# SyncE's branch to the program's end, moved ahead of its wait for the stores

## Chip, cores, metric

One core of a Trainium2 chip. The metric is the device time of the launch in microseconds (us). The kernel before takes 161.09 us (median of 3 runs, 161.05 to 161.20).

## The reference

```python
# x: float32 [32, 512, 1024]
relu_x = np.maximum(x, 0)
return np.mean(relu_x, axis=-1).astype(np.float32)      # [32, 512]
```

16384 rows of 1024 numbers: 67.11 MB are read, 64 KB are written.

## The kernel before

Each of the 128 partitions has 128 rows, of which 127 go through the main loop and one is done first, on its own. SyncE issues all loads; ScalarE and VectorE share the rows (each takes max(x, 0) and the sum in one instruction); GpSimd scales the sums; SyncE issues three stores, which all count up one semaphore, `stored`, by 16 each. The end that the change touches:

```python
    nc.sync.wait_ge(pool, 2)
    nc.sync.dma_start(out=outr[:, :j0], in_=res[:, :j0]).then_inc(stored, 16)
    nc.sync.wait_ge(dve, n_done + 2)
    nc.sync.wait_ge(pool, 4)
    nc.sync.dma_start(out=outr[:, j0:], in_=res[:, j0:]).then_inc(stored, 16)

    used = [s.num for s in (*loaded, act, dve, pool, first)]
    assert used == list(range(used[0], used[0] + len(used)))
    nc.sync.sem_clear(range(used[0], used[-1] + 1))
    nc.sync.wait_ge(stored, 48).then_inc(stored, -48)

    for e, hint in zip(hinted, hints):           # ScalarE and VectorE
        e.br_lt(flag, 1, on_true="rows_begin", on_false="rows_end").branch_hint(hint)
    nc.br("rows_end", engines=[e for e in mybir.ALL_ENGINES if e not in (h.engine for h in hinted)])
    nc.switch_bb("rows_end")
```

A program is written in blocks, and `br` is a branch to a block. Block `rows_end` follows `rows_begin` directly and is empty.

Of the kernel before, what the change touches and what calls it, by code (L numbers as in the profile page):

```python
# [25 lines left out]
def issue_ahead_of_entry_barrier(nc, n):  # L26


    entry = nc.cur_f.blocks[0].instructions
    for _ in range(n):  # L30
        body, load = next(
            (block.instructions, k)
            for block in nc.cur_f.blocks[1:]
            for k, ins in enumerate(block.instructions)
            if ins.opcode == "DMACopy"
        )
        first = body[load]
        assert first.engine == mybir.EngineType.SP and not first.sync_info.on_wait
        assert all(i.opcode in ("Drain", "EventSemaphore") or i.engine != first.engine for i in body[:load])
        del body[load]  # L40
        at = next(k for k, i in enumerate(entry) if i.engine == first.engine and i.opcode == "Drain")
        entry.insert(at, first)
# [3 lines left out]
def kernel(  # L46
# [10 lines left out]
    nc = tc.nc  # L57
# [38 lines left out]
    stored = nc.alloc_semaphore("stored")  # L96
# [115 lines left out]
    used = [s.num for s in (*loaded, act, dve, pool, first)]  # L212
    assert used == list(range(used[0], used[0] + len(used)))
    nc.sync.sem_clear(range(used[0], used[-1] + 1))
    nc.sync.wait_ge(stored, 48).then_inc(stored, -48)

    for e, hint in zip(hinted, hints):
        e.br_lt(flag, 1, on_true="rows_begin", on_false="rows_end").branch_hint(hint)
    nc.br("rows_end", engines=[e for e in mybir.ALL_ENGINES if e not in (h.engine for h in hinted)])
    nc.switch_bb("rows_end")  # L220

    issue_ahead_of_entry_barrier(nc, 2)

# [29 lines left out]
```

## Time and profile before

| | us |
|---|---|
| median of three runs | 161.09 |
| profiled run, device time | 161.36 |
| profiled run, span of the trace | 160.01 |
| of it up to the issue of the last store | 158.54 |
| from there to the end of SyncE's wait for the stores | 1.47 |

The span runs from the first to the last instruction of the kernel. The device time is longer by what follows: in the trace's semaphore records, semaphore 2 is counted up at 158.09, 158.26 and 158.67 us, and again from 160.15 us, 0.136 us after the end of SyncE's wait, to 161.458 us. I call this the closing barrier: its second part begins only when SyncE has passed its wait, in every run below. The device time is 0.095 to 0.109 us less than the last count in each profiled run of this study (161.36 here). So the time of a run is taken apart below as **the issue of the last store + the tail up to the barrier's last count - 0.10 us**; the tail of before is 161.458 - 158.543 = 2.915 us. The profile's lines for this kernel stand in the prediction.

### The profile page before, as it was taken

The page shows a single profiled execution, that of the slowest core. Times are in us where ns is not written, and L with a number is a line of the kernel's source. Part 1 is how long each engine was busy: PE and PEld are TensorE (multiplying, and loading weights), DVE is VectorE, ACT ScalarE, POOL GpSimd, SP SyncE. Part 2 cuts the span into 40 slices and gives each one's busy share as a digit, 9 for nine tenths or more (in the row PEclk, how much of TensorE's full clock was granted, in tenths as well). Part 3 has the DMA queues.
Part 4 walks back from the last instruction along what each step waited for, and adds up shares of the span by engine and source line. Part 5 has one row for each costly group of instructions (what it writes and reads, how often), then busy time and mean ns, then how long its engine had stood idle before and what let it go on. Part 6 is the DMA issues. An engine that isn't in the chain of part 4 may idle for free.

```text
span 160.0 us, 350 instructions
## 1 busy us (share of the span) xinstructions
DVE 73.5 (46%) x133; ACT 70.3 (44%) x133; POOL 1.3 (1%) x9
## 2 busy tenths in 40 slices
DVE  0000029900498005970079500894009920199975
ACT  1400029800497005950079300892009900199974
POOL 1000000000000000000000000000000000000001
DMA  9969979999799699699699699699896996989993
GB/s 393 508 279 524 459 328 524 393 393 524 311 475 524 262 524 524 262 524 524 262 524 524 262 524 524 262 524 426 360 524 262 524 524 262 477 366 460 403 411 128
DMA packets 2456, 67.18 MB, mean 420 GB/s; under 512 B 536, under 2 KB 792, under 8 KB 1176
## 3 DMA queue, kind: packets, MB, share of 16 engines
q1 hardware_dynamic: 2456, 67.18, 97.9%
HBM read 67.11 MB, written 0.07 MB: 420 GB/s over the span
## 4 chain that ended last, share of the span: by engine, by line
DMA 84%; DVE 12%; SPq 1%; issue 1%; ACT 0%; DVEq 0%
DMA rows<-in_x_dram 56%; DMA last<-in_x_dram 29%; DVE rows L20 12%; SPq L109 1%; ACT last L15 0%; DVE last L199 0%; DVEq L198 0%; SPq L115 0%
## 5 line engine op out<-in xcount | busy, mean ns | idle before, releaser
L20 DVE TENSOR_SCALAR_CACHE_REDUCE rows<-rows 128x1024 f32<-128x1024 f32 (+1 forms) x63 | 72.1, 1208 | 78.8 <-DMA rows<-in_x_dram 78.6
L15 ACT ACTIVATE rows<-rows 128x1024 f32<-128x1024 f32 x64 | 66.2, 1036 | 84.0 <-DMA rows<-in_x_dram 83.8
L15 ACT ACTIVATION_READ_ACCUMULATOR rows<-rows 128x1 f32 x64 | 12.0, 187 | 0.0
L20 DVE DVE_READ_ACCUMULATOR rows<-rows 128x1 f32 x63 | 5.2, 83 | 0.0
L168 DVE STREAM_TRANSPOSE turned<-mean 128x32 f32<-128x32 f32 x1 | 0.2, 213 | 6.1 <-ACT row L164 6.1
L164 ACT ACT_TABLE_LOAD x1 | 1.3, 1283 | 3.5 <-DMA row<-in_x_dram 3.5
L157 POOL TENSOR_SCALAR res<-sums 128x112 f32<-128x112 f32 (+1 forms) x2 | 0.5, 247 | 154.0 <-DVE rows L20 154.0
L164 ACT ACTIVATE row<-row 128x1024 f32<-128x1024 f32 x1 | 1.1, 1057 | 0.0
L20 DVE TENSOR_SCALAR_CACHE_REDUCE last<-last 128x128 f32<-128x128 f32 (+1 forms) x2 | 0.6, 318 | 0.0
L15 ACT ACTIVATE last<-last 128x448 f32<-128x448 f32 x1 | 0.6, 576 | 0.1
L199 DVE SCALAR_TENSOR_TENSOR last<-last,scale 128x259 f32<-128x259 f32 x1 | 0.4, 429 | 0.1
L142 POOL MEMSET scale<- 128x259 f32 x1 | 0.3, 314 | 0.0
L187 POOL TENSOR_SCALAR res<-part 128x1 f32<-128x1 f32 x1 | 0.3, 264 | 0.6 <-DVE rows L20 0.6
L164 ACT ACTIVATION_READ_ACCUMULATOR row<-row 128x1 f32 x1 | 0.2, 187 | 0.0
L15 ACT ACTIVATION_READ_ACCUMULATOR last<-last 128x1 f32 x1 | 0.2, 186 | 0.0
L20 DVE DVE_READ_ACCUMULATOR last<-last 128x1 f32 x2 | 0.2, 82 | 0.0
L141 POOL MEMSET mean<- 128x32 f32 x1 | 0.1, 124 | 1.5 <-POOLq L55 1.5
L237 POOL MEMSET const-bfloat16-1.0<- 128x1 bf16 x1 | 0.1, 101 | 0.0
L237 POOL MEMSET const-uint8-127<- 128x1 uint8 x1 | 0.1, 101 | 0.0
L237 POOL MEMSET const-float32-0.0<- 128x1 f32 x1 | 0.1, 98 | 0.2 <-issue 0.2
L237 POOL MEMSET const-float32-1.0<- 128x1 f32 x1 | 0.1, 99 | 0.0
L199 DVE DVE_READ_ACCUMULATOR last<-last,scale 128x1 f32 x1 | 0.1, 84 | 0.0
## 6 DMA issues: line engine op xcount, KB each, us to landing
rows<-in_x_dram SPq DMA_DIRECT2D x1, 3584.0 KB, 38.1
rows<-in_x_dram SPq DMA_DIRECT2D x1, 2048.0 KB, 42.6
rows<-in_x_dram SPq DMA_DIRECT2D x1, 1024.0 KB, 44.7
row<-in_x_dram SPq DMA_DIRECT2D x1, 512.0 KB, 3.4
rows<-in_x_dram SPq DMA_DIRECT2D x1, 512.0 KB, 45.4
last<-in_x_dram SPq DMA_DIRECT2D x1, 288.0 KB, 45.7
last<-in_x_dram SPq DMA_DIRECT2D x1, 128.0 KB, 45.4
rows<-in_x_dram SPq DMA_DIRECT2D x7, 48.8
```

Source lines behind the costliest of these rows:

```text
L15: return nc.scalar.activation(out=src, in_=src, func=ACT.Relu, accum_out=acc)
L20: return nc.vector.tensor_scalar(out=src, in0=src, scalar1=0.0, scalar2=init, op0=ALU.max, op1=ALU.add, accum_out=acc,)
L109: nc.sync.dma_start(out=dst, in_=src).then_inc(loaded[i], 16)
L141: nc.gpsimd.memset(mean0[:, :], 0.0)
L142: nc.gpsimd.memset(scale[:, :], inv).then_inc(pool, 1)
L157: nc.gpsimd.tensor_scalar(out=res[:, lo:hi], in0=sums[:, lo:hi], scalar1=inv, scalar2=0.0, op0=ALU.mult, op1=ALU.add,).then_inc(pool, 1)
L164: nc.scalar.activation(out=row0[:, :], in_=row0[:, :], func=ACT.Relu, scale=inv, accum_out=mean0[:, 0:1],).then_inc(first, 1)
L168: nc.vector.transpose(turned0[:, :], mean0[:, :]).then_inc(first, 1)
L187: nc.gpsimd.tensor_scalar(out=res[:, J - 2:J - 1], in0=part[:, 0:1], scalar1=part[:, 1:2], scalar2=inv, op0=ALU.add, op1=ALU.mult,).then_i ...
L199: nc.vector.scalar_tensor_tensor(out=last[:, 768:], in0=last[:, 768:], scalar=0.0, in1=scale[:, :], op0=ALU.max, op1=ALU.mult, accum_out=r ...
L237: nc = _bacc.Bacc("TRN2", target_bir_lowering=False, num_devices=1)
```

## The change

Its intent: SyncE has about 1 us to wait for its stores. If it branches to the program's end ahead of that wait, whatever the branch costs should lie under the wait.

```diff
     nc.sync.sem_clear(range(used[0], used[-1] + 1))
-    nc.sync.wait_ge(stored, 48).then_inc(stored, -48)
 
     for e, hint in zip(hinted, hints):
         e.br_lt(flag, 1, on_true="rows_begin", on_false="rows_end").branch_hint(hint)
     nc.br("rows_end", engines=[e for e in mybir.ALL_ENGINES if e not in (h.engine for h in hinted)])
     nc.switch_bb("rows_end")
+    nc.sync.wait_ge(stored, 48).then_inc(stored, -48)
```

## The prediction

The forecast's sum is 161.09 - 0.01 = 161.08 us, the 0.01 being taken out of the 0 to 0.03 us that the trace's gaps give for the border. From the trace's gaps alone, (a) is at most 0.03 us (an estimate: 60 - 29 ns). The 1.35 us outside the span is 161.36 - 160.01.

> **What bounds the kernel now.** I read the page first, its chain of waits and its DMA lines:
>
> ```profile
> span 160.0 us, 350 instructions
> DVE 73.5 (46%) x133; ACT 70.3 (44%) x133; POOL 1.3 (1%) x9
> ...
> q1 hardware_dynamic: 2456, 67.18, 97.9%
> HBM read 67.11 MB, written 0.07 MB: 420 GB/s over the span
> ...
> DMA 84%; DVE 12%; SPq 1%; issue 1%; ACT 0%; DVEq 0%
> ```
>
> The reader should see a program bound by its loads. The two computing engines are busy under half of the span (46% and 44%), the DMA engines 97.9% of it, and the chain that ends last is 84% DMA. Nothing in the change touches a load, so the only place where it can act is the tail. So the next view is the same chain in order of time, last pieces only (start, length, what):
>
> ```profile
> 111.55 45.74 DMA last<-in_x_dram
> 157.29 0.02 issue
> 157.31 0.06 ACT last L15
> 157.37 0.42 issue
> 157.79 0.20 ACT last L15
> 157.99 0.04 DVEq L198
> 158.03 0.04 issue
> 158.08 0.12 DVE last L199
> 158.19 0.24 issue
> 158.43 0.08 DVE last L199
> ```
>
> The last loads land about 157.3 us (those that the end hangs on), VectorE finishes the last sum at 158.51, and then comes SyncE alone. What SyncE does from there stands in the stretch of the last instructions, in the list of its waits and in the records of its wait line:
>
> ```profile
> 158.54 0.34 SPq L210 DMA_DIRECT2D out_dram<-res  x1
> ...
> SPq L215 <- SPq L215: 1.0, 1, 1.0
> ...
> L215 SPq EVENT_SEMAPHORE  x1: 17/17/17, 160.0 to 160.0; - x1
> ```
>
> SyncE issues the last store at 158.54 (0.34 us). The clearing of the semaphores follows: its record, taken straight from the trace, runs from 158.94 for 64 ns, to 159.00. SyncE then waits for the stores, line 215, for 1.0 us; the wait's own record is the last of all, 17 ns, and with it the span ends at 160.01. In between, by the trace's packet records, the store's packets run from 159.38 to 159.59 and its completion counts arrive from 159.79 to 159.98. So the tail after the last store's issue is 160.01 - 158.54 = 1.47 us, of which SyncE's own work is 0.34 + 0.06 + 0.02 us and two or three gaps of some 0.05 us. The rest is the time until the store is reported complete.
>
> [...]
>
> [...]
>
> [...] I count 33 records of SyncE in the trace, [...] and the target is the next instruction. No far target exists within the program. [...]
>
> [...] 7.5 KB moved in 0.21 us of packets, and 1.47 us from the start of the issue to the end of the wait. The change leaves all this where it is.
>
> **The change part by part.** The source moves one statement. Before, SyncE clears, waits for 48 on the stored semaphore (which the same instruction brings back to 0), then branches to the end block, which is empty. After, SyncE clears, branches to the end block, and waits there. Removed: nothing. Added: nothing. Moved: one unconditional branch, from behind a wait of 1.0 us to ahead of it. On the other four engines the order of instructions is the same in both; ScalarE and VectorE keep their conditional branch, only its line number moves by one.
>
> Now the cost of that branch. First, does it exist on the chip? The page's 350 instructions hold no unconditional branch at all: SyncE's 33 records are 18 DMA issues, 10 semaphore instructions, 4 drains and 1 clear, and lines 103 and 219, where the program branches without a condition, have no record on any engine. The two conditional ones of line 218 do have records (53 and 60 ns), so branches as such are recorded. The compiled programs agree. SyncE's has 38 words in both kernels, the same 38, and before and after differ only in that the last two have changed places: the wait and a word that is the label of the end block. A branch whose target is the next instruction is left out by the compiler, and only the label stays.
>
> Second, does the label or the left-out branch cost time? The start of this same trace has two of them on each engine (lines 248 and 103), and the first can be set against the same pair of instructions without one. From the end of a barrier's semaphore instruction to the start of the drain behind it, the records give, with a block's border between them and without one: ScalarE 74 and 75 ns, VectorE 91 and 91, GpSimd 64 and 64, TensorE 100 and 99. SyncE shows 57 ns across the border; inside a block 75, there to a drain that also has a wait, so no strict pair but no sign of a cost either. Thus a border costs 0 to 1 ns. At SyncE's second border, ahead of its third load, the gap is 60 ns where other gaps from a semaphore instruction to an issue are 29 to 47 ns: at the most generous, 60 - 29 = 31 ns could be blamed on a border.
>
> So the sum: ahead of the wait, the border adds between 0 and 0.03 us to SyncE's way from the clear (159.00) to the wait. That lies wholly under the wait, as the last count comes at 159.98 and SyncE stood ready 0.9 us before. Behind the wait, it takes away the same 0 to 0.03 us. The gain is 0 by the pairs and at most 0.03 us, 0.02% of 161.09. The span ends with the wait either way[...].
>
> I take 161.09 - 0.01 = 161.08 us.
>
> **The rivals.**
>
> (a) The loader makes something of the label, a real jump or an empty instruction, that the profiler does not record. For it: labels are in the compiled program and the trace could be silent on them. Against it: the pairs above, within 1 ns on four engines. [...]
>
> (b) The end of the program has to be fetched, and an early branch lets the fetch run beside the store. For it: this is what the author seems to want, and the 1.0 us of waiting is free time. Against it: there is no jump left to start such a fetch, and what SyncE executes behind its wait is the same fixed sequence in both. A fetch would show as part of the 1.35 us outside the span. [...]
>
> (c) The moved wait loses something: the end block is the last, other engines pass it without waiting, and one might fear that the program counts as ended before the stores have landed, which would give up to 1.47 us, 159.6 us, and a wrong result at worst. Against it: SyncE still executes the same wait, and all of its later work stands behind it. [...]
>
> (d) The run's own spread. Three runs of before lie from 161.05 to 161.20, and the profiled one at 161.36. The loads move 67 MB at 420 GB/s and a change of 0.1% in that rate is 0.16 us, five times the largest gain that I can derive. So whatever difference is measured, it will most likely be this.
>
> **Range and chances.** The centre is before's median less 0.01. The spread of before (0.15 us over three runs, 0.3 with the profiled run) gives the range: about 0.25 us below and 0.3 above, hence 160.83 to 161.38. [...] For 2% the time would have to move by 3.2 us, more than twice the whole tail behind the last issue; nothing that the change touches is that large. Hence 1% for faster, 1% for slower (a disturbed set of runs), 98% for within 2%.
>
> **What would show it right or wrong.** In the profile after: again 350 instructions; SyncE again 33 records with no branch among them; the clear again about 0.06 us after the issue's end, the last record again a 17 ns semaphore instruction on SyncE, now of line 220 instead of 215, about 1.47 us after the last issue began, and a wait of 1.0 us ahead of it. A branch record between the clear and the wait would contradict the reading that the branch does not exist. A tail shorter than 1.4 us, or a measured time that falls while the span stays the same, would speak for (a) or (b). If the times of the two kernels, taken in the same rounds, differ by more than 0.1 us beyond their spread, the step that says the border costs nothing is wrong. If the load part ahead of 157.3 us differs instead, that is rival (d) and says nothing of the change.

## The result, and the profile after

After: 161.25 us (median of 6 runs, 161.09 to 161.68). Before, in the same rounds and with the first three runs: 161.14 us (6 runs, 161.05 to 161.60). The ratio is 1.0004, with a 95% interval of 0.9987 to 1.0021: the same. (Ratios here and below are the mean time of one kernel's fast runs over that of the other's of the same rounds, so not quite the ratio of the medians.)

The page of the changed kernel, its head, DMA lines and chain of waits:

```profile
span 160.0 us, 350 instructions
DVE 73.5 (46%) x133; ACT 70.3 (44%) x133; POOL 1.3 (1%) x9
...
q1 hardware_dynamic: 2456, 67.18, 97.9%
...
DMA 84%; DVE 12%; SPq 1%; issue 1%; ACT 0%; DVEq 0%
```

There is the same span, the same 350 instructions, the same busy times. Next the end of the chain in order of time (start, length, what):

```profile
111.57 45.69 DMA last<-in_x_dram
157.26 0.02 issue
...
158.41 0.08 DVE last L199
```

Then, from the last instructions, SyncE's waits and the records of line 220, to which the wait has moved:

```profile
158.52 0.34 SPq L210 DMA_DIRECT2D out_dram<-res  x1
...
SPq L220 <- SPq L220: 1.0, 1, 1.0
...
L220 SPq EVENT_SEMAPHORE  x1: 17/17/17, 160.0 to 160.0; - x1
```

(The list of waits names a line as its own releaser; by the semaphore records it is the store that releases it, as the wait's record starts 17 ns after the last count of `stored`, before and after.) Everything from the last store's issue on repeats to a few nanoseconds: the wait ends 1.474 us after the issue (before: 1.471), and the barrier's last count comes 1.443 us after that (before: 1.444). The tail is 2.917 us against 2.915. No branch of SyncE is recorded between the clear and the wait.

### The profile page after: what moved, and what is told of

Its sections match the earlier page's. It is cut to its first block, busy times and chain, and to the rows that moved or that the text cites. A ratio compares the mean times of both kernels' runs of the same rounds, so it can differ in the third digit from the quotient of the medians.

```text
span 160.0 us, 350 instructions
## 1 busy us (share of the span) xinstructions
DVE 73.5 (46%) x133; ACT 70.3 (44%) x133; POOL 1.3 (1%) x9
## 4 chain that ended last, share of the span: by engine, by line
DMA 84%; DVE 12%; SPq 1%; issue 1%; ACT 0%; DVEq 0%
DMA rows<-in_x_dram 56%; DMA last<-in_x_dram 29%; DVE rows L20 12%; SPq L109 1%; ACT last L15 0%; DVE last L199 0%; DVEq L198 0%; SPq L115 0%
```

## The experiments

The theory: the moved branch does not exist on the chip, because its target is the next instruction, so there was nothing to hide. The rivals were that its label costs something that the profile does not show, and that branches or their instruction fetches are free or cannot be hidden anyway, so that not even a real one would gain. All twelve runs gave correct results. Each was compared with runs of the kernel before on its own chip: chip 11 for the noise, the labels and the eight jumps, chip 15 for the four jumps and the changed kernel once more, chip 8 for the single jumps near and far, and chip 0 for the last run.

### Noise: before against itself

Edit: none.

> The kernel before, unchanged, against itself: the noise that every comparison has to beat. All theories: ratio 1.000, with an interval of some 0.1 to 0.2% to each side; single runs from 161.0 to 161.7 us, as in the comparison of after with before (161.05 to 161.68). If two identical kernels differ by as much as after and before did (ratio 1.0004, medians 0.11 us apart), that difference says nothing of the change.

Measured: 161.35 us (5 runs, 161.21 to 161.55) against 161.18 us (11 runs); ratio 1.0012 (0.9999 to 1.0025); tail 2.925 us. Two identical kernels differ by 0.17 us in their medians, more than after and before (0.11 us). Spans and times of single runs move together (161.04 with a span of 159.7, 161.49 with 160.1), while in the profiled runs the tail is the same within 10 ns. So the spread lies ahead of the last store, as far as the traces show, and the tail is the better gauge for a change that can act only there.

### The changed kernel once more

Edit: none; this is after, run beside the kernels with 4 jumps.

> The changed kernel once more, beside the others on one chip. Theory: it is before in all but the place of a label; ratio to before 1.000, within the 0.0012 by which before differed from itself. Rival [...]: not to be told from that noise in the times; in the trace the time from the wait's end to the closing barrier's last count would be shorter than before's 1.444 us by as much.

Measured: 161.16 us (6 runs) against 161.25 us (11 runs, one of them at 162.07); ratio 0.9989 (0.9972 to 1.0006); tail 2.917 us, from the wait's end to the barrier's last count 1.444 us, exactly before's. Where the first comparison had after slower by 0.0004, this one has it faster by 0.0011. Both are noise. The rival's small gain, at most 0.03 us by the gaps of the prediction, is not in the tail.

### A hundred labels behind the wait

A label is the word that marks the start of a block in an engine's compiled program. Condensed against the kernel before:

```diff
+    nc.switch_bb("gate")
     nc.sync.wait_ge(stored, 48).then_inc(stored, -48)
-    nc.br("rows_end", engines=[e for e in mybir.ALL_ENGINES if e not in (h.engine for h in hinted)])
+    nc.br("rows_end", engines=[e for e in mybir.ALL_ENGINES if e != nc.tensor.engine])
+    hops = 100
+    nc.tensor.br(f"hop{hops - 1}")
+    for h in range(hops):
+        nc.switch_bb(f"hop{h}", parent=None)
+        nc.tensor.nop(nofuse=True)
+        nc.tensor.br(f"hop{h - 1}" if h else "rows_end")
+    nc.switch_bb("rows_end", parent=None)
```

(The other engines branch to `gate` in place of `rows_end` at the end of the loop's block; the compiler drops the `nop`, here and in the runs with 8 and 4 jumps. SyncE's compiled program then holds 101 labels in a row behind its wait.)

> The kernel before with 100 more empty blocks behind SyncE's wait for the stores. The compiler leaves out SyncE's branches and keeps one label for each, so that 101 labels stand behind the wait in place of 1 (TensorE, which has nothing to do, jumps backwards through these blocks so that they are not merged away; it does so at about 2 us). Theory (a label is nothing on the chip): span 160.0 us, no new record on SyncE, measured time 161.1 to 161.3 us, ratio 1.000 within 0.002. Rival (the loader turns a label into a jump or an empty instruction that the profile hides): [...] with the span unchanged as the added time lies behind its last record.

Measured: 161.12 us (5 runs); ratio 0.9995 (0.9982 to 1.0008); tail 2.923 us. The page's head and two records, SyncE's wait and TensorE's jumps through the same blocks:

```profile
span 160.1 us, 451 instructions
...
L220 SPq EVENT_SEMAPHORE  x1: 17/17/17, 160.1 to 160.1; - x1
...
L227 PEldq COMPARE_BRANCH  x100: 163/163/168, 2.2 to 24.5; - x100
```

The 101 instructions more are TensorE's real jumps (100 on this line, one on another; those 100 start 0.225 us apart on average, (24.5 - 2.2) / 99). SyncE has its 33 records as ever, and its wait is the last. A hundred labels changed its tail by 8 ns, within the 10 ns that before differs from itself, so one label costs at most about 0.2 ns (my estimate: 8 ns and the 10 ns of noise, over 100). At the 31 ns that the prediction could at most blame on a border, a hundred would be 3.1 us; the rival is excluded.

### Eight real jumps, behind and ahead of the wait

In before and after, the branch to the next instruction left no record. Here 7 blocks are laid out in the reverse order of their visit, so that no target is the next instruction, and 8 jumps of SyncE are then recorded (both variants in one, condensed; the other engines go on as in the last experiment):

```diff
+    nc.switch_bb("gate")
+    nc.sync.wait_ge(stored, 48).then_inc(stored, -48)      # behind: the jumps follow the wait
     ...
+    hops = 7
+    nc.sync.br(f"hop{hops - 1}")
+    for h in range(hops):
+        nc.switch_bb(f"hop{h}", parent=None)
+        nc.sync.nop(nofuse=True)
+        nc.sync.br(f"hop{h - 1}" if h else "rows_end")
+    nc.switch_bb("rows_end", parent=None)
+    nc.sync.wait_ge(stored, 48).then_inc(stored, -48)      # ahead: the wait stands here instead
```

> SyncE takes 8 real jumps BEHIND its wait for the stores (7 blocks laid out in the reverse order of their visit, so that no target is the next instruction). Theory: real jumps do cost time and stand in the trace, by ScalarE's and VectorE's records of line 218 53 to 60 ns each, with the gap to the next 0.06 to 0.11 us: span and time grow by 0.5 to 0.9 us, to 161.6 to 162.0 us, ratio 1.003 to 1.0055. Rival (branches are free on SyncE in any case, so the change could not gain even with a real one): no growth, 161.1 us.

Measured: 162.25 us (5 runs); ratio 1.0067 (1.0054 to 1.0080), above what was expected. Tail 4.068 us, 1.153 us longer than before's. The records of the wait and of seven of the jumps:

```profile
L220 SPq EVENT_SEMAPHORE  x1: 17/17/17, 160.0 to 160.0; - x1
...
L227 SPq COMPARE_BRANCH  x7: 33/33/33, 160.2 to 161.1; - x7
```

Real jumps of SyncE are recorded (these 7 and the first, on line 223), so their absence in before and after means something. Each record, a compare-and-branch though the jump has no condition, is 33 ns, but from one jump to the next it is 142 ns. I had sized the step from the records of the other engines, at 0.06 to 0.11 us, which was too little.

> The same 8 real jumps AHEAD of the wait. Theory: 0.5 to 0.9 us fits into the 0.97 us in which SyncE only waits for the stores, so nothing is seen: span 160.0 us, the wait itself shorter (0.1 to 0.5 in place of 1.0 us), time 161.1 to 161.3 us, ratio 1.000. Rival (moving a jump ahead of the wait costs as much as it gives, for instance because the store's transfer is started later): as long as with the jumps behind, 161.6 to 162.0 us. That pair is what the change would have been, had its branch been a real one, times 8.

Measured: 161.32 us (6 runs); ratio 1.0015 (1.0001 to 1.0028). Tail 3.135 us, of which 0.220 us is more than before's.

```profile
L226 SPq COMPARE_BRANCH  x7: 33/33/33, 158.9 to 159.8; - x7
...
L228 SPq EVENT_SEMAPHORE  x1: 17/17/17, 159.9 to 159.9; - x1
```

Placing the jumps ahead of the wait takes 4.068 - 3.135 = 0.933 us out of the tail. The expectation that all of it would be hidden failed by the mis-sized jump: 8 jumps of 142 ns are 1.14 us and do not fit into the 0.98 us of waiting. The last count of `stored` came at 159.70 us, but SyncE reached its wait only at 159.91.

### Four jumps, which fit

Edit: as above with `hops = 3`.

> 4 real jumps behind the wait. Theory, with 0.142 us each from the runs with 8 jumps: 0.57 us more, 161.7 us, ratio 1.0035. Rival (the first 8 cost what they did for another reason than their number[...]): not half of the 1.09 us that 8 jumps added to the span.

Measured: 161.76 us (6 runs); ratio 1.0030 (1.0012 to 1.0048). Tail 3.509 us, 0.594 us more than before's, about half of the 1.153 us of eight jumps.

> 4 real jumps ahead of the wait, 0.57 us, which now fit wholly under the 0.98 us of waiting (8 jumps took 1.14 us and left 0.2 us of tail exposed). Theory: tail from the last store's issue to the end of the wait 1.47 us as in before, wait shortened to about 0.4 us, ratio 1.000. Rival (a jump ahead of the wait is never wholly hidden): tail longer by 0.1 us or more, as with 8.

Measured: 161.17 us (6 runs); ratio 0.9998 (0.9978 to 1.0019). SyncE's waits, the line of the stores:

```profile
SPq L228 <- SPq L228: 0.5, 1, 0.5
```

The wait has shrunk from 1.0 to 0.5 us, as the jumps now use up its first half. The wait ends 1.471 us after the issue of the last store, to the nanosecond as before. The tail is 2.940 us, 0.025 us longer than before's; that rest lies behind the wait (1.469 us to the barrier's last count, in place of 1.444), and all of it ahead of the barrier's first count there (0.160 us after the wait's end, in place of 0.136).

### One real jump, near and far

The conditional form of a branch, with a flag that always sends SyncE over instructions never executed (one, or 700; condensed):

```diff
+    spflag = nc.alloc_registers("spflag", engines=[nc.sync.engine])
+    nc.regs_mov(spflag, 1)
     ...
+    nc.sync.br_lt(spflag, 1, on_true="never", on_false="rows_end")
+    nc.switch_bb("never", parent=None)
+    for _ in range(1):                                     # or 700
+        nc.sync.nop(cycle_cnt=10)
+    nc.sync.br("rows_end")
+    nc.switch_bb("rows_end", parent=None)
```

> One real jump BEHIND the wait: SyncE jumps over one instruction that is never executed (its flag register holds 1). Theory: the runs with 8 jumps gave 0.142 us from one jump to the next, so one jump adds 0.14 us behind the wait: 161.3 us, ratio 1.001, hardly clear of the noise in the times, but in the trace a branch record behind the wait, and 0.14 to 0.2 us from the wait's end to where the program's own closing barrier begins more than before. It is the control for the far jump.

> The same one real jump AHEAD of the wait: what the change would be with a branch that exists. Theory: 0.14 us under a wait of 0.98 us, nothing left of it: tail from the last store's issue to the end of the wait 1.47 us, time 161.1 to 161.3 us, ratio 1.000. Against its twin with the jump behind the wait it should gain about 0.14 us, a tenth of a per cent, which the times may not resolve.

Measured, behind: 161.34 us (5 runs), ratio 1.0013 (0.9999 to 1.0026), tail 3.098 us. Ahead: 161.24 us (5 runs), ratio 1.0003 (0.9989 to 1.0016), tail 2.949 us. The times cannot tell these from before, but the tails can: a single real jump behind the wait costs 0.183 us, ahead of it 0.034 us. Had the moved branch been a real one of this kind, moving it would have been worth 0.149 us, or 0.09%.

> One jump BEHIND the wait over 700 instructions that are never executed [...]. [...] Theory: the near jump costs 0.14 us, the far one that plus a fetch from memory; from the store's own receipt in this trace (some 0.2 to 0.9 us for one way of it) I guess 0.5 to 3 us more than the near jump: 161.8 to 164.5 us. Rival (distance doesn't matter, so the change could not gain by a fetch either): as the near jump, 161.3 us.

Measured: 163.82 us (5 runs, 163.71 to 164.45); ratio 1.0173 (1.0155 to 1.0192). Tail 5.659 us, 2.561 us more than with the near jump. The two kernels differ only in how many instructions are jumped over, 1 or 700, so in this pair the distance of the target is what costs the 2.561 us, and the rival falls. (No distance between was tried.) The trace's DMA records show traffic of the queue for instructions at that place. The jump's record ends at 159.817 us; a packet of 8192 bytes on the queue for instructions runs from 160.697 to 161.264 us; and the barrier's next count comes at 162.591 us, where in the near twin it comes 0.212 us after the jump's record. So the packet itself is only 0.57 us of the stall: 0.88 us pass before it and 1.33 us between it and that count, and what fills these is not shown. (A second such packet, at 163.022 us, comes when SyncE has gone on already.) In the two traces of the first comparison, before and after, the last packet on that queue comes 0.09 us ahead of the span's start, in none of the four traces of these kernels later than 0.05 us, and in the near twins' there is none in the tail either.

> The same far jump AHEAD of the wait: the case in which the change's idea should pay. Theory: of the far jump's cost F, up to 0.98 us lies under the wait for the stores, so it is faster than its twin by the smaller of F and some 0.9 to 1.0 us: 161.1 us if F is under 0.98 us, 160.1 us + F otherwise. Rival (the fetch waits for the same engines as the store's transfer, or holds it up): gain under 0.3 us.

Measured: 163.21 us (4 runs, 162.92 to 163.38); ratio 1.0122 (1.0105 to 1.0138). Tail 4.613 us. Its jump, SyncE's wait and the queues:

```profile
L223 SPq COMPARE_BRANCH  x1: 45/45/45, 159.2 to 159.2; - x1
...
SPq L229 <- SPq L229: 2.6, 1, 2.6
...
q1 hardware_dynamic: 2456, 67.18, 96.9%
q14 instruction: 1, 0.01, 0.0%
```

Here is a trap in reading: the 2.6 us before line 229 are booked as a wait for the stores. The last of their counts came at 160.143 us, while the wait was passed at 161.83. In the near twin, with the same wait at the same place, the wait's record starts 17 ns after the last count. So SyncE lacked something else, and the queue "instruction" in the DMA lines is the hint (its packet runs from 160.127 to 160.760 us): I take it for the instruction behind the jump. What fills the 1.07 us from the packet's end to the wait is not shown. The tail is shorter than its twin's by 1.046 us, about the length of the wait and a little over, and the rest of the stall stays exposed. The medians, however, were only 0.61 us apart; in the profiled runs the last store was issued 0.46 us later here than in the twin (158.70 against 158.24). One more run was to settle that:

> The far jump ahead of the wait, once more and on its own. Its first run gained 0.6 us in the medians on its twin with the jump behind the wait, where the traces of the two show 1.05 us between the last store's issue and the closing barrier's last count (5.66 against 4.61 us); its loads had come to their end some 0.3 us later than those of before. Theory (that is chance of this load of the program, as with the kernel before against itself, 0.17 us): the last store is issued about 158.4 us as in before, and the time is 158.4 + 4.61 - 0.10 = 162.9 us, ratio 1.0105. Rival (the program with the far jump ahead really delays the loads by 0.3 us): 163.2 us again, ratio 1.0122.

Measured: 162.95 us (4 runs, 162.77 to 163.02); ratio 1.0109 (1.0092 to 1.0126); last store issued at 158.459 us, tail 4.600 us. So the late loads did not come again when the same program was loaded on another chip, and the far jump gains 163.82 - 162.95 = 0.87 us (medians from two different chips) to 1.06 us (tails) by standing ahead of the wait.

### All tails side by side

| kernel | last store's issue to the wait's end, us | wait's end to the barrier's last count, us | tail, us |
|---|---|---|---|
| before, twice | 1.471, 1.478 | 1.444, 1.447 | 2.915, 2.925 |
| after, twice | 1.474, 1.473 | 1.443, 1.444 | 2.917, 2.917 |
| 101 labels behind | 1.477 | 1.446 | 2.923 |
| 1 jump behind / ahead | 1.475 / 1.484 | 1.623 / 1.465 | 3.098 / 2.949 |
| 4 jumps behind / ahead | 1.475 / 1.471 | 2.034 / 1.469 | 3.509 / 2.940 |
| 8 jumps behind / ahead | 1.470 / 1.666 | 2.598 / 1.469 | 4.068 / 3.135 |
| far jump behind / ahead, twice | 1.476 / 3.146, 3.133 | 4.183 / 1.467, 1.467 | 5.659 / 4.613, 4.600 |

A jump ahead of the wait leaves about 0.02 us between the wait's end and the last count (1.465, 1.469 and 1.469 us with 1, 4 and 8 jumps, against before's 1.444); its cause was not found. No variant beats before, and none was built to: each only adds to a program which, before and after, has no jump to hide.

## Why the prediction was right

**The branch does not exist.** The prediction had this right. It is shown: real jumps of SyncE do leave records (8 of them in the runs with 8), and neither kernel has one there.

**The label costs nothing that was measured.** The prediction allowed 0 to 0.03 us. (Its upper end took 29 ns as the smallest of the other gaps; the trace has 30, which changes nothing.) A hundred labels changed the tail by 8 ns, so the lower end was right, and the gain of 0.01 us that it took off the median was a concession to a cost of zero.

**The tail stays.** Predicted were 350 instructions, 33 records of SyncE, the clear about 0.06 us after the issue's end, a wait of 1.0 us and about 1.47 us from the issue to the last record; measured were 350, 33, 0.051, 1.0 and 1.474. Of the 1.44 us from the store's issue to its last count (1.44 to 1.45 in all profiled runs), 0.84 lie ahead of the first packet and 0.39 behind the end of the last one. As the change leaves the store alone, nothing hangs on it.

**Rival (a), a hidden jump,** is excluded by the labels: 101 of them changed the tail by 8 ns. A real jump of SyncE cost 142 ns in the rows of 8 and 183 ns alone behind the wait.

**Rival (b), a fetch of the program's end,** is excluded for these two kernels, since no instruction packet moves during their tails (the last comes 0.09 us ahead of the span), and the barrier behind SyncE's wait takes 1.444 and 1.443 us in them. Where SyncE does jump over 700 instructions, a stall of 2.56 us and a packet on that queue within it are measured.

**Rival (c), a wait that loses its force,** did not occur: results are correct and SyncE's wait ends the span in both. The instruction records show no barrier behind the kernel; the semaphore records do, and its second part starts 0.136 us after the end of SyncE's wait in both kernels.

**Rival (d), the run's own spread,** is what the difference was, as the tails are 2.915 and 2.917 us. That the time fell into the range is owed to the width given for this spread; the 0.01 us of forecast gain was far below what the times could test. After's median was 0.17 us above the predicted 161.08, and identical kernels differed by 0.17 us in another set. The profiled runs issued their last store anywhere from 158.24 to 158.70 us. Why it varies with each loading of the program was not examined and stays open.

## What to carry to other kernels

Before paying attention to where a branch stands, look for it in the records: here the branch to the block that comes next left none, and moving it changed the tail by 2 ns (2.915 to 2.917 us). A real jump on SyncE was worth hiding under the wait (0.15 us each), the one over 700 instructions more so (about 1 us of 2.7), and only about as much was hidden as the wait is long (1.05 us of the far jump under 0.98 us of waiting). When runs scatter by more than the effect, split the time at the last point that the change cannot touch: here the load part scattered by 0.46 us, while the tail repeated to 10 ns.
